# Sums of squares on VectorE alone, and weight pieces split in halves in the first two mixers

## The chip, the core and the metric

The kernel runs on one core of a Trainium2 chip. TensorE does the matrix products (PE in the profile; PEld is its loading of stationary operands), VectorE (DVE), ScalarE (ACT) and GpSimd (POOL) the elementwise work, and SyncE's queue issues the loads. The metric is device microseconds of one execution. The kernel before takes 1027.95 us, the median of 3 runs (1027.83 to 1028.59).

## The reference

Two transformer blocks run one after the other on 256 tokens of width 1024, all in float32. Each has a mixer and a feed-forward part (the second block has two of both), and ahead of each stands an RMS norm:

```
def rmsnorm(x, g):
    return x * lax.rsqrt(jnp.mean(x * x, axis=-1) + EPS) * g

# first block                             # second block
h = h + mixer(rmsnorm(h, g0))             h = h + hgrn2(rmsnorm(h, g0))
u = conv(rmsnorm(h, g1) @ w_up)           h = h + swiglu(rmsnorm(h, g1))
h = h + (silu(gate) * val) @ w_down       h = h + moba(rmsnorm(h, g2))
x = rmsnorm(h, g_final)                   h = h + swiglu(rmsnorm(h, g3))
...
```

The first mixer projects to queries, keys and gates, runs an attention that keeps the 64 best keys of an index score and a latent attention, and merges both through gates. The second is a gated linear recurrence (HGRN2), whose output is normed too; the third is block attention. Widths: the first projection has 3816 columns, the feed-forward inner width is 2816.

## The kernel before

**Tiling.** The residual `h` lies feature-major: 128 partitions by 8 feature blocks by 256 tokens. A product in float32 is made of three products in fp32r: each operand is split into a rounded high part H and the rest L, and H·H, H·L and L·H are summed in PSUM (`mm3`, L511; `proj_w`, L680, does the same with H and L of the tokens side by side, 512 columns). Tokens X, H and L, come from the end of the stage before; weights are split when they have been loaded.

**Weights.** `Weights` (L445) loads a matrix in pieces of up to 1024 elements per partition, 512 KB each. `__getitem__` (L461) splits a whole piece in two instructions: ScalarE copies it to H (`r<-f`, L467), VectorE subtracts H to give L (`r<-f,r`, L468). Pools: 15 raw pieces (`f4`), 23 tiles of H or L (`r4`), so pieces are loaded and split ahead.

**The end of a stage.** `end` (L634) closes each mixer and the first two feed-forward parts. The new values stand in four PSUM banks `accs`, two feature blocks each. Per bank, VectorE adds it to `h` (L650), ScalarE makes X's H (L652) and VectorE X's L (`SCALAR_TENSOR_TENSOR r<-h,vec,r`, or `r<-h,fs,r`, L653). Then `squares` (L571) sums the squares of the eight blocks: ScalarE squares `h` in four tiles of 128x512, and three additions make one tile of them, on GpSimd unless an engine is given. `over_partitions` (L589) folds its two halves (128x256) on the same engine, and eight small TensorE products with `ones` sum over partitions. `mean_rsqrt` (L599) makes 1/rms of it in ten VectorE instructions of 128x2, and `bcast` (L559) spreads it to all partitions: two VectorE instructions `f<-pack,fs`, two TensorE products, a ScalarE copy. The next stage's products use the X that isn't normed yet, and are scaled by 1/rms when they leave PSUM. So TensorE goes on from stage to stage as soon as X is there; the sum and the broadcast stand in its queue among products of the next stage. The end of the convolutional feed-forward part calls `squares` twice (L655, L658): once for the final norm of the first block, and once with its gains, on VectorE, for the first norm of the second block.

**Five such ends** are spoken of below: that of the first mixer (near 195 us), of the first feed-forward part (near 382), of the second mixer (near 529), of the second feed-forward part (near 722) and of the third mixer (near 829). In the second mixer, GpSimd also adds up the squares of the recurrence's output, once for each pair of heads but the first (L1324).

**Order.** The code only records operations (`Trace.add`, L209). `schedule` (L295) then orders them for all engines at once: at each step the engine that is free first takes, of the operations whose inputs are there by a table of prices (`price`, L257), the one recorded first. An operation with `ahead` tiles, such as the split of a weight piece, so fills gaps as long as tiles are free. `nc.floor` (L250) makes every operation recorded while it is set wait for one given operation. Each engine executes its list strictly in order. GpSimd's price is 1000 + 4 ns per element for two inputs, VectorE's 69 + 1.042 (L278 to L288).

Of the kernel before, what the change touches and what calls it, by code (L numbers as in the profile page):

```python
# [9 lines left out]
F32 = mybir.dt.float32  # L10
# [181 lines left out]
class Trace:  # L192
    def __init__(self, nc):
        self.nc, self.ops, self.kinds, self.floor = nc, [], {}, None
        for name in ("tensor", "vector", "scalar", "gpsimd", "sync"):
            setattr(self, name, Engine(self, name))
# [248 lines left out]
class Weights:  # L445
# [15 lines left out]
    def __getitem__(self, k):  # L461
        p = k // self.per
        k0 = p * self.per
        if p not in self.parts:
            nc, raw = self.b.nc, self.fetch(p)
            H, L = (nc.tile("r4", raw.shape, ahead=True) for _ in range(2))
            nc.scalar.activation(H, raw, AF.Copy)  # L467
            nc.vector.tensor_tensor(L, raw, H.bitcast(F32), op=ALU.subtract)  # L468
            self.parts[p] = H, L
        H, L = self.parts[p]  # L470
        return H[:, k - k0, :], L[:, k - k0, :]
# [10 lines left out]
class Builder:  # L482
# [87 lines left out]

    def squares(self, scale=None, eng=None):  # L571

        nc = self.nc
        tot = None
        for i in range(4):
# [7 lines left out]
            if tot is None:  # L583
                tot = sq
            else:
                (eng or nc.gpsimd).tensor_tensor(tot, tot, sq, op=ALU.add)
        return self.over_partitions(tot, eng or nc.gpsimd)

    def over_partitions(self, tot, eng):  # L589

        ss, v = self.ps(2), self.t("f1", SEQ)
        eng.tensor_tensor(v, tot[:, 0], tot[:, 1], op=ALU.add)
        for t in range(2):
# [40 lines left out]
    def end(self, accs, g, scale=None, norm=None):  # L634
# [21 lines left out]
        if norm is not None:  # L656

            ss, v = self.squares(norm, nc.vector), self.t("fs", 2)  # L658
            nc.vector.tensor_tensor(v, r, r, op=ALU.mult)
# [542 lines left out]
    def mixer2(self, X):  # L1202
# [103 lines left out]
        def outs(p, sc, it, og):  # L1306
# [14 lines left out]
            else:  # L1321
                o2 = self.t("f2", 2, SEQ)
                A_.activation(o2, po, AF.Square)
                G.tensor_tensor(sq, sq, o2, op=ALU.add)  # L1324

        for p in range(4):
            sc = scores(p, *front(p))
            outs(p, sc, *sides(p))
        ro = self.bcast(self.mean_rsqrt(self.over_partitions(sq, V)))
        accs = self.new_accs()  # L1330
# [80 lines left out]
def build(tc, a, out, stop=None):  # L1411
    with ExitStack() as ctx:
# [9 lines left out]

        X = b.setup()
        X = b.mixer1(X)
        end = b.nc.last("gpsimd")
        b.late_setup()
# [10 lines left out]
        if stopped("x2"):  # L1437
            return
        X = b.mixer2(X)
        if stopped("h3"):  # L1440
            return
# [33 lines left out]
```

## Time and profile before

The profiled execution took 1028.07 us, its first to last instruction (the span) 1026.3 us.

| | |
|---|---|
| median of 3 runs | 1027.95 us |
| profiled execution | 1028.07 us |
| its span | 1026.3 us |
| TensorE, matrix products busy | 999.1 us, 97% |
| VectorE busy | 774.5 us, 75% |
| ScalarE busy | 577.7 us, 56% |
| GpSimd busy | 42.6 us, 4% |
| granted TensorE clock, mean | 0.999 |

PE's busy time counts products from start to a modelled end, so small gaps are hidden in it; what the table can't tell is when an engine waited and for whom. That is read from the waits and from the order of time in single stretches. Names are the program's, with buffer numbers left out: `ps` is a PSUM bank, `r` a tile of H or L, `f` a float32 tile, `fs` a small one, `h` the residual. All recorded instructions have line 434, so stretches and names tell them apart.

### The profile page before, as it was taken

The numbers are of one execution on the slowest core, as the hardware profiler recorded it, in microseconds if no ns is written. First come the engines' busy times: TensorE is split into PE (matmuls) and PEld (weight loads), VectorE is DVE, ScalarE is ACT, GpSimd is POOL, SyncE is SP. The second block draws the span as 40 slices with busy tenths as digits, with TensorE's granted clock in tenths as the row PEclk, the third lists the DMA queues.
The fourth block names the chain that finished last, engine by engine and source line by source line (L and its number), as shares of the span: only waits on it lengthen the run. The fifth ranks groups of instructions, "written<-read, shape, count | busy, mean of one in ns | idle before, by whom it ended". The sixth has DMA issues, their size and how long they took to land.

```text
span 1026.3 us, 18746 instructions
## 1 busy us (share of the span) xinstructions
PE 999.1 (97%) x7526; PEld 907.1 (88%) x7526; DVE 774.5 (75%) x1434; ACT 577.7 (56%) x960; POOL 42.6 (4%) x41
## 2 busy tenths in 40 slices
PE   7999999999999999999999999999999999999996
PEld 5887899889999998999998999999889988888885
DVE  6998578699888889876878776767846586576774
ACT  7886646556656576444565445455554655545432
POOL 1000000210000002000011000000200020000000
PEclk9999999999999999999999999999999999999999
DMA  9245367377465663644554765657354745556501
GB/s 333 80 145 184 103 190 225 124 242 242 153 207 187 201 199 90 184 146 138 160 178 144 244 192 180 199 171 226 104 161 149 232 148 153 183 176 196 164 1 42
DMA packets 130152, 173.90 MB, mean 169 GB/s; under 512 B 5842, under 2 KB 112730, under 8 KB 129936
## 3 DMA queue, kind: packets, MB, share of 16 engines
q1 hardware_dynamic: 129312, 169.31, 52.5%
q0 software_dynamic: 752, 3.38, 1.0%
q8 instruction: 59, 0.97, 0.4%
q14 instruction: 29, 0.24, 0.1%
HBM read 171.61 MB, written 2.63 MB: 170 GB/s over the span
## 4 chain that ended last, share of the span: by engine, by line
PE 89%; DVE 9%; issue 1%; ACT 1%; DMA 1%; POOL 0%; DVEq 0%; POOLq 0%; ACTq 0%
PE ps L434 89%; DVE r L434 4%; DVE f L434 3%; DVE fs L434 1%; DVE h L434 1%; DMA f<-in_conv_w_dram 1%; ACT f L434 1%; POOL f L434 0%; ACT r L434 0%; DVEq L434 0%; DVE lb L434 0%; POOLq L434 0%; ACTq L434 0%; POOLq L1462 0%
## 5 line engine op out<-in xcount | busy, mean ns | idle before, releaser
L434 PE MATMUL ps<-r,r 128*128 128x256 f32 (+2 forms) x5998 | 926.4, 314 | 8.1 <-DVE r L434 7.5
L434 PEld LDWEIGHTS ps<-r,r 128*128 128x128 f32 x5998 | 834.3, 190 | 81.9 <-DVE r L434 11.1
L434 DVE TENSOR_TENSOR r<-f,r 128x1024 fp32r<-128x1024 f32 (+3 forms) x369 | 414.3, 1150 | 69.6 <-ACT r L434 33.9
L434 ACT ACTIVATE r<-f 128x1024 fp32r<-128x1024 f32 (+3 forms) x373 | 351.1, 980 | 118.9 <-PE ps L434 54.9
L434 ACT ACTIVATE f<-ps 128x256 f32<-128x256 f32 (+5 forms) x226 | 85.5, 424 | 190.5 <-PE ps L434 190.2
L434 DVE TENSOR_TENSOR f<-ps,f 128x256 f32<-128x256 f32 (+1 forms) x178 | 76.0, 460 | 80.5 <-ACT f L434 64.5
L434 DVE TENSOR_TENSOR f<-f,f 128x512 f32<-128x512 f32 (+3 forms) x153 | 100.6, 658 | 12.1 <-ACT f L434 5.5
L434 ACT ACTIVATE f<-f 128x512 f32<-128x512 f32 (+5 forms) x82 | 45.1, 551 | 49.4 <-DVE f L434 48.9
L434 POOL TENSOR_TENSOR f<-f,f 128x512 f32<-128x512 f32 x18 | 26.9, 1494 | 768.5 <-ACT f L434 459.1
L434 DVE SCALAR_TENSOR_TENSOR f<-f,cw,f 128x255 f32<-128x255 f32 (+1 forms) x88 | 38.3, 480 | 10.8 <-ACT f L434 10.7
L434 PE MATMUL ps<-f,f 128*64 128x128 f32 (+4 forms) x320 | 46.3, 330 | 0.1
L434 PEld LDWEIGHTS ps<-f,f 128*64 128x64 f32 (+3 forms) x320 | 35.7, 168 | 6.7 <-issue 2.1
L434 PE MATMUL ps<-pack,f 128*128 128x128 f32 (+2 forms) x165 | 27.5, 293 | 6.5 <-DMA f<-in_conv_w_dram 3.6
L434 ACT ACTIVATE f<-f,fs 128x256 f32<-128x256 f32 (+3 forms) x50 | 24.3, 489 | 16.7 <-DVE fs L434 16.5
L434 ACT ACTIVATE f<-f,vec,cw 128x256 f32<-128x256 f32 x44 | 23.9, 594 | 16.7 <-DVE f L434 16.7
L434 PEld LDWEIGHTS ps<-pack,f 128*128 128x128 f32 (+2 forms) x165 | 20.2, 147 | 11.1 <-DVE f L434 4.8
L434 DVE CUSTOM_DVE_ANT_0 f<-ps,f 128x256 f32<-128x256 f32 (+1 forms) x48 | 17.8, 399 | 14.2 <-PE ps L434 14.1
L434 ACT ACTIVATE f<-ps,fs 128x512 f32<-128x512 f32 (+3 forms) x28 | 15.9, 597 | 19.9 <-PE ps L434 18.8
L434 DVE SCALAR_TENSOR_TENSOR r<-h,vec,r 128x256 fp32r<-128x256 f32 x32 | 23.3, 763 | 2.0 <-ACT r L434 2.0
L434 ACT ACTIVATE r<-h,vec 128x256 fp32r<-128x256 f32 x32 | 14.5, 500 | 15.9 <-DVE h L434 15.9
L434 DVE TENSOR_TENSOR f<-f,fs 128x512 f32<-128x512 f32 (+6 forms) x46 | 16.6, 389 | 7.2 <-PE ps L434 6.7
L434 PEld LDWEIGHTS ps<-f 128*32 128x32 f32 (+2 forms) x880 | 14.0, 114 | 4.3
(85 smaller groups left out, 244.2 us busy)
## 6 DMA issues: line engine op xcount, KB each, us to landing
f<-in_ffn_w_dram SPq DMA_DIRECT2D x132, 512.0 KB, 4.2
f<-in_w_up_dram SPq DMA_DIRECT2D x44, 512.0 KB, 4.7
f<-in_hgrn_w_in_dram SPq DMA_DIRECT2D x32, 512.0 KB, 4.3
f<-in_w_in_dram SPq DMA_DIRECT2D x26, 512.0 KB, 4.9
f<-in_moba_w_in_dram SPq DMA_DIRECT2D x24, 512.0 KB, 4.5
f<-in_w_down_dram SPq DMA_DIRECT2D x22, 512.0 KB, 4.2
f<-in_w_out_dram SPq DMA_DIRECT2D x8, 512.0 KB, 3.9
f<-in_hgrn_w_out_dram SPq DMA_DIRECT2D x8, 512.0 KB, 3.3
```

The costliest lines, as they stand in the source:

```text
L434: getattr(getattr(self.nc, op.eng), op.fn)(*args, **kwargs)
```

## The change

Three things are changed. (1) `squares` and `over_partitions` no longer take an engine: all additions are on VectorE, that of the recurrence's squares too. GpSimd keeps memsets, its DMA issues and one scaling at the very end. (2) In `squares`, the three additions get a floor: they may not come ahead of the last VectorE operation recorded before the call. (3) While `nc.fine` is set, which is in the first and the second mixer, a weight piece is split in two halves on each engine, by rows of the piece where it has more than one, else by columns. The operation that `store_rel` waits for is now the last TensorE operation of the first mixer, not the last GpSimd one.

```diff
     def __getitem__(self, k):
...
             H, L = (nc.tile("r4", raw.shape, ahead=True) for _ in range(2))
-            nc.scalar.activation(H, raw, AF.Copy)
-            nc.vector.tensor_tensor(L, raw, H.bitcast(F32), op=ALU.subtract)
+            if nc.fine:
+                cut = raw.shape[1] > 1
+                n = raw.shape[1] if cut else self.n
+                for c in (slice(0, n // 2), slice(n // 2, n)):
+                    c = (slice(None), c) if cut else (slice(None), slice(None), c)
+                    nc.scalar.activation(H[c], raw[c], AF.Copy)
+                    nc.vector.tensor_tensor(L[c], raw[c], H[c].bitcast(F32), op=ALU.subtract)
+            else:
+                nc.scalar.activation(H, raw, AF.Copy)
+                nc.vector.tensor_tensor(L, raw, H.bitcast(F32), op=ALU.subtract)
...
-    def squares(self, scale=None, eng=None):
+    def squares(self, scale=None):
         nc = self.nc
-        tot = None
+        tot, before = None, nc.last("vector")
...
-                (eng or nc.gpsimd).tensor_tensor(tot, tot, sq, op=ALU.add)
-        return self.over_partitions(tot, eng or nc.gpsimd)
+                nc.floor = before
+                nc.vector.tensor_tensor(tot, tot, sq, op=ALU.add)
+                nc.floor = None
+        return self.over_partitions(tot)
...
-        eng.tensor_tensor(v, tot[:, 0], tot[:, 1], op=ALU.add)
+        self.nc.vector.tensor_tensor(v, tot[:, 0], tot[:, 1], op=ALU.add)
...
-            ss, v = self.squares(norm, nc.vector), self.t("fs", 2)
+            ss, v = self.squares(norm), self.t("fs", 2)
...
-                G.tensor_tensor(sq, sq, o2, op=ALU.add)
+                V.tensor_tensor(sq, sq, o2, op=ALU.add)
...
+        b.nc.fine = True
         X = b.mixer1(X)
-        end = b.nc.last("gpsimd")
+        b.nc.fine = False
+        end = b.nc.last("tensor")
...
+        b.nc.fine = True
         X = b.mixer2(X)
+        b.nc.fine = False
```

In numbers: 23 additions leave GpSimd (18 of 128x512, 5 of 128x256) and come to VectorE; 90 weight pieces are split in 180 instructions on ScalarE and 180 on VectorE (82 of them were 128x1024, 4 128x976, 2 128x768, 2 128x512). TensorE's instructions are the same, in another order.

Since a scheduler sets the order, the diff doesn't show it. Three places do.

First place, VectorE at the end of the first mixer, from the addition of the last bank to `h` (`h_170`); `r_83` there is X's last L, `r<-f,r` are weight pieces, `fs_136<-ps_153` takes the sum of squares. Before:

```order
L434 TENSOR_TENSOR h_170<-ps_154,h_170 128x512
L434 TENSOR_TENSOR r_87<-f_69,r_95 128x1024
L434 SCALAR_TENSOR_TENSOR r_83<-h_170,vec_182,r_83 128x256 x2
L434 TENSOR_TENSOR r_92<-f_65,r_79 128x1024
L434 TENSOR_TENSOR r_81<-f_64,r_80 128x1024
L434 TENSOR_TENSOR f_107<-ps_157,f_116 128x256
L434 TENSOR_TENSOR f_107<-ps_159,f_121 128x256
L434 TENSOR_SCALAR fs_136<-ps_153 128x2
```

Now (`h_170` from `ps_153`, X's last L is `r_81`):

```order
L434 TENSOR_TENSOR h_170<-ps_153,h_170 128x512
L434 TENSOR_TENSOR r_89<-f_64,r_76 128x1024
L434 SCALAR_TENSOR_TENSOR r_81<-h_170,vec_182,r_81 128x256 x2
L434 TENSOR_TENSOR f_109<-f_109,f_103 128x512
L434 TENSOR_TENSOR f_109<-f_109,f_110 128x512
L434 TENSOR_TENSOR r_94<-f_60,r_78 128x1024
L434 TENSOR_TENSOR f_109<-f_109,f_104 128x512
L434 TENSOR_TENSOR f_105<-ps_158,f_123 128x256
L434 TENSOR_TENSOR f_119<-f_109 128x256
L434 TENSOR_TENSOR f_105<-ps_159,f_118 128x256
L434 TENSOR_TENSOR r_87<-f_67,r_90 128x1024
L434 TENSOR_SCALAR fs_136<-ps_160 128x2
```

The three additions and the fold of the halves (`f_119<-f_109`) now stand between X's last L and the sum, with one weight piece among them; GpSimd had them before.

Second place, VectorE at the end of the first feed-forward part, where two sums are made. Before, the second sum's additions (`f_103`) and fold (`f_120`) stood behind X's L, around the first steps of the first 1/rms (`fs_138` to `fs_130`):

```order
L434 TENSOR_TENSOR f_103<-f_103,f_104 128x512
L434 TENSOR_TENSOR r_90<-f_68,r_76 128x1024
L434 TENSOR_TENSOR f_103<-f_103,f_107 128x512
L434 TENSOR_SCALAR fs_138<-ps_159 128x2
L434 TENSOR_TENSOR f_103<-f_103,f_102 128x512
L434 TENSOR_SCALAR fs_148<-fs_138 128x2
L434 TENSOR_TENSOR f_120<-f_103 128x256
L434 TENSOR_TENSOR fs_130<-fs_148 128x2
L434 SCALAR_TENSOR_TENSOR fs_130<-fs_130,fs_138 128x2
L434 SCALAR_TENSOR_TENSOR fs_130<-fs_130 128x2
L434 SCALAR_TENSOR_TENSOR fs_148<-fs_130,fs_148 128x2
L434 TENSOR_TENSOR fs_130<-fs_148 128x2
```

Now the second sum (`f_104`, fold `f_125`) stands behind the end of that 1/rms (`fs_135`), around its broadcast (`f_126`, `f_116` from `pack_174`), and takes `ps_160` after the first products of it:

```order
L434 SCALAR_TENSOR_TENSOR fs_148<-fs_148,fs_138 128x2
L434 SCALAR_TENSOR_TENSOR fs_148<-fs_148 128x2
L434 SCALAR_TENSOR_TENSOR fs_135<-fs_148,fs_135 128x2
L434 TENSOR_TENSOR f_104<-f_104,f_109 128x512
L434 TENSOR_TENSOR fs_130<-fs_135 128x2
L434 TENSOR_SCALAR f_126<-pack_174,fs_135 128x128
L434 TENSOR_TENSOR f_104<-f_104,f_106 128x512
L434 TENSOR_SCALAR f_116<-pack_174,fs_135 128x128
L434 TENSOR_TENSOR f_104<-f_104,f_108 128x512
L434 TENSOR_TENSOR f_125<-f_104 128x256
L434 SCALAR_TENSOR_TENSOR h_170<-h_170,vec_182,f_120 128x256 x2
L434 SCALAR_TENSOR_TENSOR fs_130<-ps_160,fs_130 128x2
```

Third place, VectorE at the start of the first mixer: `r_78` is the L of the first weight piece, `r_77` to `r_81` are X's L, `f_105` and `f_106` the transposed second half of the tokens, `r_84` the second piece. Before:

```order
L434 TENSOR_TENSOR r_78<-f_59,r_76 128x976
L434 TENSOR_TENSOR r_77<-f_103,r_77 128x2x128
L434 TENSOR_TENSOR r_79<-f_103,r_79 128x2x128
L434 TENSOR_TENSOR r_80<-f_104,r_80 128x2x128
L434 TENSOR_TENSOR r_81<-f_104,r_81 128x2x128
L434 TENSOR_TENSOR f_105<-ps_158,vec_182 128x512
L434 TENSOR_TENSOR f_106<-ps_159,vec_182 128x512
L434 TENSOR_TENSOR r_84<-f_61,r_82 128x976
```

Now, from the tokens' second half on (the first half of piece one stands where the whole piece stood, X's four L's of the first half behind it as before):

```order
L434 TENSOR_TENSOR f_105<-ps_158,vec_182 128x512
L434 TENSOR_TENSOR f_106<-ps_159,vec_182 128x512
L434 TENSOR_TENSOR r_78<-f_59,r_76 128x488
L434 TENSOR_TENSOR r_77<-f_105,r_77 128x2x128
L434 TENSOR_TENSOR r_79<-f_105,r_79 128x2x128
L434 TENSOR_TENSOR r_80<-f_106,r_80 128x2x128
L434 TENSOR_TENSOR r_81<-f_106,r_81 128x2x128
L434 TENSOR_TENSOR r_84<-f_61,r_82 128x488 x2
```

The second half of piece one moved behind the transposed second half of the tokens, and piece two behind X's L of it.

## Rows read from the trace of the kernel before

**Rows 1.** The page's first part: busy us of each engine, its share, its instructions.

```profile
PE 999.1 (97%) x7526; PEld 907.1 (88%) x7526; DVE 774.5 (75%) x1434; ACT 577.7 (56%) x960; POOL 42.6 (4%) x41
```

**Rows 2.** Stretches: length, busy of PE, PEld, DVE, ACT, POOL; PEclk, DMA share, GB/s.

```profile
15.50:42.00 26.50, 26.50 (x138) 22.69 (x140) 26.50 (x117) 24.41 (x49) 0.54 (x1) 1.00 0.56 198
42.00:60.50 18.50, 16.23 (x102) 14.02 (x99) 18.36 (x72) 16.90 (x36) 0.00 (x0) 1.00 0.32 94
194.70:210.00 15.30, 13.82 (x95) 11.41 (x93) 14.76 (x27) 8.59 (x16) 6.91 (x6) 1.00 0.28 84
398.00:529.00 131.00, 130.91 (x1799) 124.70 (x1800) 101.85 (x200) 65.25 (x103) 4.50 (x3) 1.00 0.52 161
529.00:542.00 13.00, 11.25 (x66) 9.04 (x66) 12.78 (x18) 8.46 (x15) 5.26 (x4) 1.00 0.25 80
```

**Rows 3.** Waits of PE, then PEld, 190 to 845 us: total, times, longest.

```profile
PE ps L434 <- DVE r L434: 7.0, 7, 1.8
PE ps L434 <- POOL f L434: 0.7, 1, 0.7
PE ps L434 <- DVE f L434: 0.6, 1, 0.6
...
PEld ps L434 <- DVE r L434: 10.2, 10, 2.0
PEld ps L434 <- DVE f L434: 1.6, 4, 0.8
PEld ps L434 <- POOL f L434: 0.9, 1, 0.9
```

**Rows 4.** Timeline at the first mixer's end: start, us, instructions [idle before <-releaser].

```profile
195.31 3.75 DVE L434 SCALAR_TENSOR_TENSOR r<-h,vec,r 128x256 fp32r<-128x256 f32 x4
195.79 2.98 POOL L434 TENSOR_TENSOR f<-f,f 128x512 f32<-128x512 f32 x2 [179.55 <-DVE r L434]
201.24 3.76 PE L434 MATMUL ps<-r,r 128*128 128x512 f32 x19 [1.40 <-DVE r L434]
```

**Rows 5.** Timeline at the second mixer's end, VectorE and GpSimd.

```profile
530.85 0.89 DVE L434 SCALAR_TENSOR_TENSOR r<-h,vec,r 128x256 fp32r<-128x256 f32 x2
533.99 1.91 DVE L434 SCALAR_TENSOR_TENSOR r<-h,vec,r 128x256 fp32r<-128x256 f32 x2
534.09 1.52 POOL L434 TENSOR_TENSOR f<-f,f 128x512 f32<-128x512 f32 x1 [15.55 <-ACT f L434]
```

**Rows 6.** Groups by shape: shapes and count | busy us, mean ns | idle before, releasers.

```profile
L434 DVE TENSOR_TENSOR r<-f,r 128x1024 fp32r<-128x1024 f32 x312 | 380.6, 1238 | 55.5 <-ACT r L434 19.9 <-issue 16.3 <-PE ps L434 16.3
L434 ACT ACTIVATE r<-f 128x1024 fp32r<-128x1024 f32 x312 | 317.9, 1051 | 67.0 <-PE ps L434 54.9 <-issue 11.9
L434 DVE TENSOR_TENSOR f<-f,f 128x512 f32<-128x512 f32 x137 | 95.1, 694 | 12.0 <-ACT f L434 5.5 <-PE ps L434 4.6
L434 POOL TENSOR_TENSOR f<-f,f 128x512 f32<-128x512 f32 x18 | 26.9, 1494 | 768.5 <-ACT f L434 459.1 <-DVE r L434 308.8 <-POOL f L434 0.2
L434 ACT ACTIVATE r<-f 128x512 fp32r<-128x512 f32 x43 | 27.1, 632 | 51.3 <-DVE f L434 51.3
L434 DVE TENSOR_TENSOR f<-f 128x256 f32<-128x256 f32 x6 | 2.5, 422 | 1.2 <-POOL f L434 1.2
```

**Rows 7.** Timeline of VectorE: weight pieces split one behind the other.

```profile
82.01 5.76 DVE L434 TENSOR_TENSOR r<-f,r 128x1024 fp32r<-128x1024 f32 x5
```

**Rows 8.** Timeline, sum of squares to broadcast, after the first mixer.

```profile
206.08 0.14 DVE L434 TENSOR_SCALAR fs<-ps 128x2 f32<-128x2 f32 x1
209.38 0.71 PE L434 MATMUL ps<-f,ones 128*128 128x128 f32 x4
```

**Rows 9.** Timeline of PE, three waits inside the first mixer.

```profile
15.46 11.70 PE L434 MATMUL ps<-r,r 128*128 128x488 f32 x51 [0.52 <-DVE r L434]
50.54 2.82 PE L434 MATMUL ps<-pack,f 128*96 128x128 f32 x24 [1.60 <-DVE f L434]
60.48 0.70 PE L434 MATMUL ps<-pack,f 128*128 128x128 f32 x4 [0.67 <-DVE f L434]
```

More of the change, by code (lines that the diff above doesn't have):

```diff
@@ L193, in __init__ @@
     def __init__(self, nc):
-        self.nc, self.ops, self.kinds, self.floor = nc, [], {}, None
+        self.nc, self.ops, self.kinds, self.floor, self.fine = nc, [], {}, None, False
         for name in ("tensor", "vector", "scalar", "gpsimd", "sync"):
@@ L585, in squares, with over_partitions @@
             else:
-                (eng or nc.gpsimd).tensor_tensor(tot, tot, sq, op=ALU.add)
-        return self.over_partitions(tot, eng or nc.gpsimd)
-    def over_partitions(self, tot, eng):
+                nc.floor = before
+                nc.vector.tensor_tensor(tot, tot, sq, op=ALU.add)
+                nc.floor = None
+        return self.over_partitions(tot)
+    def over_partitions(self, tot):
         ss, v = self.ps(2), self.t("f1", SEQ)
-        eng.tensor_tensor(v, tot[:, 0], tot[:, 1], op=ALU.add)
+        self.nc.vector.tensor_tensor(v, tot[:, 0], tot[:, 1], op=ALU.add)
         for t in range(2):
@@ L1328, in mixer2 @@
             outs(p, sc, *sides(p))
-        ro = self.bcast(self.mean_rsqrt(self.over_partitions(sq, V)))
+        ro = self.bcast(self.mean_rsqrt(self.over_partitions(sq)))
         accs = self.new_accs()
```

## The prediction

> **What bounds the kernel now.** I read the page's first part before anything else. TensorE's products fill 97% of the span and its loads 88%, VectorE 75%, ScalarE 56%, GpSimd 4% [rows 1]: TensorE is the bound, and a change that takes no product away can only win what TensorE waits. So the next view is the table by stretch, to see where those waits are. In the second mixer PE is busy for 130.91 of 131.00 us; at the end of the first mixer it is 13.82 of 15.30, and at the end of the second 11.25 of 13.00, with VectorE busy for 14.76 and 12.78 there [rows 2]. The reader is to see that the gaps sit at the ends of stages, and that VectorE is full at just these places though it is at 75% over all. The third view, who waited for whom, gives them their sum. From 190 us to 845 us, which holds all five ends, the products waited 8.3 us (7.0 for an `r` of VectorE, 0.7 for GpSimd's `f`, 0.6 for VectorE's), and the loads 10.2, 1.6 and 0.9 us for the same three [rows 3]. The load waits are the fuller measure, since a product's end is modelled and covers the start of a gap; of their 1.6 us on VectorE's `f` I count the longest, 0.8, and leave the three short ones, which stand at the broadcasts and stay. So between **8.3 and 11.9 us** of the span are stalls at the five ends.
>
> The last view is the order of time there, to see what makes VectorE late. At the end of the first mixer four `SCALAR_TENSOR_TENSOR r<-h` (X's L) take 3.75 us, and from 0.5 us after their start GpSimd adds for 2.98 us; PE then waits 1.40 us for an `r` [rows 4]. At the end of the second mixer two of them take 0.89 us where GpSimd is idle, and the next two, 3 us later and of the same shape, take 1.91, with an addition of GpSimd (1.52 us) from 0.1 us after their start [rows 5]. So VectorE's instruction is held by about as long as GpSimd's takes: at 0.89 a pair, the four would have taken 1.78, not 3.75. GpSimd's additions are not a help beside VectorE; they stop it while TensorE waits for the next L.
>
> **The change part by part.**
>
> *Additions off GpSimd.* The four L's at the end of the first mixer are done 2.0 us earlier (3.75 less 1.78), which is more than the 1.40 us that PE waited there and about the 1.8 us of the longest load wait. The other ends have the same pattern, and the wait for GpSimd's own `f` (0.7 to 0.9) goes with them. What is late next is TensorE: its products are there. I take the middle of the two measures, **10.1 us won**.
>
> *The same additions on VectorE.* An addition of 128x512 is 0.69 us there against 1.49 on GpSimd, a fold 0.42 [rows 6]: three and one are 2.5 us for a sum, 18 and 5 are 14.6 us in all. The floor puts them behind X's last L, so they can't delay what TensorE waits for first. Queued behind them on VectorE are weight pieces, of which some are ready ahead, and the ten steps of 1/rms. These end in the broadcast, for which PE waits in its order: from the sum to the broadcast's product there were 3.3 us, with one weight piece among them [rows 8]. The new order sets products of the next stage between, enough for a chain of that length by the steps above, but with little to spare. Below nothing I see no reason; above, a whole sum (2.5 us) could come out at each end. I take 0.2 us at each of four ends, which is nearest to their short broadcast waits of before, together 0.8.
>
> *The end with two sums.* There the second sum's additions stood among the first steps of the first 1/rms; now they stand behind its end, so the second broadcast comes later, by up to a sum's 2.5 us. Behind it wait the evictions of the second mixer's first products, not the products themselves, until the broadcast's place in PE's order. Between 0 and 2.5 us; I take 0.4, near the lower end, because one whole projection and most of another stand in PE's order between the two.
>
> *The recurrence's squares.* Three additions of 0.69 us move to VectorE in a stretch where it is busy for 101.85 of 131.00 us and PE waits for nothing [rows 2]. Nothing. If that cover were gone it would be 2.1 us.
>
> *Splitting in halves.* A piece costs VectorE 1.238 us alone, but five in a row take 5.76, so each hides 0.11 behind the one before [rows 6, 7]. Two halves at 0.69 are 1.38 less that overlap, so a split costs 0.03 (1.38 less 0.11 less 1.24) to 0.14 us. On ScalarE it is 2 x 0.632 less 1.051, 0.21, or 0.10 with the same overlap. For 90 pieces this is 3 to 13 us on VectorE and 9 to 19 on ScalarE, beside a TensorE that waits little. It counts only where both engines are full: from 15.5 to 60.5 us VectorE is busy for 44.86 of 45.00 us, and ScalarE for 41.31 [rows 2]. Fourteen pieces are split there in VectorE's order; at 0.06 us each, between the bounds, that is **0.8 us lost**, since PE waits for VectorE at the end of that stretch (1.60 and 0.67 us [rows 9]). Gained at the start: PE's first long run begins after a wait of 0.52 us for the second piece's L [rows 9], and in the new order it has products of both token halves to do before that. I book none of it, because VectorE, not PE, is what is late at 50 us. In the second mixer the halves find no wait to shorten (0.09 us [rows 2]).
>
> The Trainium skill ("Perfetto Trace Analysis", section "Optimizing Scalar/DVE Operations") speaks against the halves: an instruction carries a fixed access cost, about 60 ns on VectorE and 93 on ScalarE in SBUF, and where the engine is saturated larger operations do better. By it fourteen splits would cost 2.1 us if both lay in series, and the sum would end 1.3 us higher.
>
> *The floor of `store_rel`* moves two small loads behind the first broadcast; the one product that needs them stands thirty products further on in PE's order. Nothing, or some tenths.
>
> *Sum.* 10.1 less 0.8 (four broadcasts), 0.4 (two sums) and 0.8 (halves) is 8.1 us. Against the profiled execution's 1028.07 us, 0.12 above the median, that gives **1020.0 us**.
>
> **The rivals.**
>
> *The sum becomes the wait (slower).* Each end's additions, 2.5 us on VectorE, come between X and the broadcast. If PE reaches the broadcast's place sooner than VectorE gets there, it waits by the whole sum at each end, and once more where there are two: six sums, 15 us. Against a gain of 10.1 and with the halves' 0.8 that is 1033.8; at two thirds of it 1028.8. It decides against the change as soon as more than 1.5 us of each sum comes out. For it: GpSimd ran these additions in parallel. Against: VectorE gets back about as much as it is given (2.0 us on four L's alone, against 2.5), and the order was made with VectorE's prices, which are near its durations.
>
> *The halves take it back.* The first mixer is bound by VectorE to 60 us, and a new order there may cost what it likes: at the upper bounds fourteen splits are 2.0 us on VectorE and 2.9 on ScalarE, 4.9 in series, 4.1 more than booked: **1024.1 us**. For it: 44.86 of 45.00. Against: PE has other products to fill with in the new order.
>
> *The halves gain too.* If the earlier first half moves the whole chain, the waits of 0.52, 1.60 and 0.67 us [rows 9] go, 2.8 us: **1017.2 us**. Against: VectorE has more to do there, not less.
>
> *The change doesn't do what it says.* If X's L's are slow for another reason, say because ScalarE's H comes late, taking GpSimd away frees only the 0.7 to 0.9 us that PE waited for GpSimd itself, and the time stays at **1027**. Against: rows 5, the same instruction at both speeds a few us apart.
>
> **How the numbers follow.** Chances: forecast 0.62, halves take it back 0.15, halves gain 0.10, the sum becomes the wait 0.07, no effect 0.06. The range reaches down to all load waits won with some of the start's 0.52 (1028.07 less 11.9 less 0.5, 1015.7), and up to the smaller measure with the two-sum end at its bound and half of the halves' 4.9 (8.3 less 0.8, 2.5 and 2.5 is 2.5: 1025.5): 1015.5 to 1025.5. It holds the forecast's case, the second and most of the third. A measurement of this kernel can tell about 0.2%, 2 us, from no change, so below 1025.9 counts as faster: 0.85 (forecast, most of the second case, the third); within 2 us of before 0.09; slower 0.06.
>
> **What would show it.** In the trace of the changed kernel, the four L's at the first mixer's end should take some 1.7 us, not 3.75, the waits of PE for `r` at the five ends should be near nothing (below 2 us together, from 8.3), and GpSimd should have no additions. New waits would stand at the broadcasts (`f<-pack,fs` as releaser) if the sum is late. From 10 us to 95 us the trace should be at most 1 us longer. Wrong is the prediction if the L's are as slow as before, if the broadcasts wait over 1 us each, or if the first mixer's end moves by more than 2 us either way.

## The result and the profile after

The changed kernel takes **1019.08 us** (median of 4 runs, 1018.50 to 1019.43) where the kernel before takes 1028.15 beside it: a ratio of 0.991, 95% interval 0.9896 to 0.9923. It is 9.1 us faster; 1020.0 was predicted, with a range of 1015.5 to 1025.5. The total came out as forecast, but two terms of the sum were mis-sized in opposite directions, and the experiments below are mostly about these.

The first part of the page of the changed kernel (busy us, share, instructions), and its chain by engine:

```profile
PE 1000.9 (98%) x7526; PEld 909.1 (89%) x7526; DVE 775.2 (76%) x1547; ACT 584.2 (57%) x1050; POOL 9.4 (1%) x18
...
PE 97%; DVE 1%; DMA 1%; ACT 0%; issue 0%; POOLq 0%
```

Against [rows 1], VectorE is busy for 0.7 us more although it does 113 instructions more, GpSimd for 33 us less. The same stretches as [rows 2], in the changed kernel (length, then busy time and count of PE, PEld, DVE, ACT, POOL, then clock, DMA share, GB/s):

```profile
15.50:42.00 26.50, 26.50 (x127) 22.13 (x125) 26.02 (x127) 24.82 (x62) 1.06 (x2) 1.00 0.55 188
42.00:60.50 18.50, 18.46 (x107) 15.58 (x107) 18.50 (x65) 17.36 (x36) 0.00 (x0) 1.00 0.35 114
194.70:210.00 15.30, 15.30 (x113) 13.81 (x112) 14.49 (x27) 9.01 (x17) 0.68 (x2) 1.00 0.40 126
398.00:529.00 131.00, 130.79 (x1809) 124.15 (x1808) 104.56 (x233) 66.26 (x130) 0.00 (x0) 1.00 0.50 161
529.00:542.00 13.00, 13.00 (x94) 11.36 (x93) 12.72 (x23) 8.90 (x17) 0.00 (x0) 1.00 0.22 66
```

At the two stage ends PE is now busy for the whole stretch (15.30 of 15.30, 13.00 of 13.00), and does 113 and 94 products there, before 95 and 66. Note the second row: PE is "busy" for 18.46 us instead of 16.23, with only five products more. Each product counts from its start to its modelled end, so a slow row can look full: 32 products of 64x256 take 5.93 us there, one every 0.185, without an idle time between them, where before 16 took 2.00, one every 0.125. This row says nothing of progress; the times at which things happen, further down, do.

The waits from 190 to 845 us [rows 3]: for the products there is no row left at all. For the loads (total, times, longest) there are these two:

```profile
PEld ps L434 <- issue: 1.4, 4, 0.6
PEld ps L434 <- DVE f L434: 0.6, 2, 0.4
```

The waits for VectorE's `r` and for GpSimd's `f` are gone, and all but 0.6 us of those for VectorE's `f`: 8.3 us by the products, 12.1 by the loads (10.2, 1.6 and 0.9, less the 0.6 left). The time line at the first mixer's end, VectorE's four L's (answering [rows 4]) and PE up to the broadcast (answering [rows 8]):

```profile
198.02 1.71 DVE L434 SCALAR_TENSOR_TENSOR r<-h,vec,r 128x256 fp32r<-128x256 f32 x4
...
207.38 0.16 DVE L434 TENSOR_SCALAR fs<-ps 128x2 f32<-128x2 f32 x1
...
206.41 0.31 PE L434 MATMUL ps<-ones,f 128*32 128x1 f32 x16
206.64 7.27 PE L434 MATMUL ps<-r,r 128*128 128x256 f32 x41
213.75 0.61 PE L434 MATMUL ps<-f,ones 128*128 128x128 f32 x4
```

Four L's take 1.71 us, before 3.75. From the sum to the broadcast's product there are now 6.4 us (207.38 to 213.75), before 3.3, yet nothing waits: 41 products stand between, and none of these rows has an idle time in brackets. At the second mixer's end [rows 5] both pairs now take the same:

```profile
529.32 0.88 DVE L434 SCALAR_TENSOR_TENSOR r<-h,vec,r 128x256 fp32r<-128x256 f32 x2
...
532.46 0.88 DVE L434 SCALAR_TENSOR_TENSOR r<-h,vec,r 128x256 fp32r<-128x256 f32 x2
```

Over the whole run, all 32 L's of this form lie between 476 and 488 ns; before, between 472 and 1604. The groups by shape that answer [rows 6] (count | busy us, mean ns | idle before):

```profile
L434 DVE TENSOR_TENSOR r<-f,r 128x1024 fp32r<-128x1024 f32 x230 | 276.1, 1220 | 59.2 <-PE ps L434 22.6 <-ACT r L434 20.7 <-issue 14.4
L434 ACT ACTIVATE r<-f 128x1024 fp32r<-128x1024 f32 x230 | 233.7, 1051 | 59.7 <-PE ps L434 53.6 <-issue 6.1
L434 DVE TENSOR_TENSOR r<-f,r 128x512 fp32r<-128x512 f32 x201 | 132.6, 687 | 15.4 <-ACT r L434 15.1
L434 DVE TENSOR_TENSOR f<-f,f 128x512 f32<-128x512 f32 x155 | 106.7, 689 | 10.5 <-ACT f L434 6.7 <-PE ps L434 1.4
```

82 whole pieces are gone and 162 halves of 512 have come (other halves are smaller), at the price that [rows 6] gave for a half, and the 18 additions that VectorE took over cost 0.69 us each, as booked.

**What went the other way** is the first mixer. Its landmarks in the changed kernel (PE's first group with conv_w's transposes; VectorE's MAX8, which carry the choice of keys, with shortest, median and longest ns and first and last start; a wait of PE behind them; the first addition to h at the end):

```profile
8.01 2.44 PE L434 MATMUL ps<-pack,f 44*128 44x44 f32 x11 [4.57 <-DMA f<-in_conv_w_dram]
...
L434 DVE MAX8 fs<-f x16: 404/419/425, 53.7 to 80.5; 128x8 f32<-128x256 f32 x16
...
98.28 0.70 PE L434 MATMUL ps<-pack,f 128*128 128x128 f32 x4 [0.81 <-DVE f L434]
...
194.53 0.69 DVE L434 TENSOR_TENSOR h<-ps,h 128x512 f32<-128x512 f32 x1 [1.00 <-PE ps L434]
```

The same four in the kernel before:

```profile
7.00 2.44 PE L434 MATMUL ps<-pack,f 44*128 44x44 f32 x11 [3.59 <-DMA f<-in_conv_w_dram]
...
L434 DVE MAX8 fs<-f x16: 406/420/433, 47.4 to 78.1; 128x8 f32<-128x256 f32 x16
...
95.43 0.70 PE L434 MATMUL ps<-pack,f 128*128 128x128 f32 x4 [0.61 <-DVE f L434]
...
191.82 0.69 DVE L434 TENSOR_TENSOR h<-ps,h 128x512 f32<-128x512 f32 x1 [1.00 <-PE ps L434]
```

The first mixer's end comes 2.7 us later. Of this 1.0 us is there from the start: PE waits for the transfer of conv_w and goes on at 7.00 us in one execution and at 8.01 in the other, and both kernels wait for it alike. Counted from there, the first mixer takes 184.82 us before and 186.52 after: **1.7 us lost**. The first MAX8 comes 5.3 us later by the same count, the last 1.4.

### The profile page after: what moved, and what is told of

Its sections match the earlier page's. It is cut to its first block, busy times and chain, and to the rows that moved or that the text cites. A ratio compares the mean times of both kernels' runs of the same rounds, so it can differ in the third digit from the quotient of the medians.

```text
span 1017.7 us, 18892 instructions
## 1 busy us (share of the span) xinstructions
PE 1000.9 (98%) x7526; PEld 909.1 (89%) x7526; DVE 775.2 (76%) x1547; ACT 584.2 (57%) x1050; POOL 9.4 (1%) x18
## 4 chain that ended last, share of the span: by engine, by line
PE 97%; DVE 1%; DMA 1%; ACT 0%; issue 0%; POOLq 0%
PE ps L434 97%; DMA f<-in_conv_w_dram 1%; DVE f L434 0%; DVE fs L434 0%; ACT f L434 0%; ACT r L434 0%; DVE r L434 0%; POOLq L1477 0%
## 5 line engine op out<-in xcount | busy, mean ns | idle before, releaser
L434 ACT ACTIVATE r<-f 128x1024 fp32r<-128x1024 f32 (+3 forms) x463 | 359.0, 827 | 114.5 <-DVE f L434 54.5
L434 DVE TENSOR_TENSOR f<-f,f 128x512 f32<-128x512 f32 (+4 forms) x171 | 112.3, 658 | 10.6 <-ACT f L434 6.7
L434 PE MATMUL ps<-f,f 128*64 128x128 f32 (+4 forms) x320 | 49.3, 332 | 0.2
L434 ACT ACTIVATE f<-f,fs 128x256 f32<-128x256 f32 (+3 forms) x50 | 24.3, 488 | 16.9 <-DVE fs L434 16.8
L434 PE MATMUL ps<-f 128*32 128x16 f32 (+3 forms) x880 | 17.7, 191 | 0.0
L434 DVE SCALAR_TENSOR_TENSOR r<-h,vec,r 128x256 fp32r<-128x256 f32 x32 | 14.3, 482 | 2.1 <-ACT r L434 2.1
```

Source lines behind the costliest of these rows:

```text
L434: getattr(getattr(self.nc, op.eng), op.fn)(*args, **kwargs)
```

## The experiments

The theory was the prediction's: GpSimd's additions hold VectorE's instructions that read two operands from SBUF, and at the stage ends TensorE waits for these; the halves cost a little where VectorE is full. The rivals were that GpSimd was only a slow link in the chain, and that the halves gain, or take much back.

**The additions alone.** The halves are left out.

```diff
-        b.nc.fine = True
         X = b.mixer1(X)
-        b.nc.fine = False
...
-        b.nc.fine = True
         X = b.mixer2(X)
-        b.nc.fine = False
```

> The changed kernel without the halves: all additions of squares on VectorE, every weight piece split by one instruction per engine. The theory of the prediction (the additions earn the time at the stage ends, the halves cost some 0.8 us): 1018.3 us, ratio to before 0.990. Rival, the halves take much back (up to 1.6 us of the first mixer's loss between 98 and 112 us, and as much in the second): 1015.5 to 1017.5. Rival, the halves gain too: 1021 to 1023.

1017.15 us (1017.09 to 1017.34), before 1028.84, ratio 0.9886 (0.9872 to 0.9899). The additions earn 11.7 us, and the halves take 1.9 of them back (1019.08 less 1017.15). The intervals allow some 1.5 us either way, but the traces say the same: counted from conv_w's transposes to the last instruction, the kernel before takes 1019.3 us, this one 1007.6 and the changed one 1009.6, so 11.7 are earned and 2.1 taken back.

They are also earned where they were looked for. From the first addition to h at one end to that at the next, the trace here is 2.0, 2.6, 2.7 and 1.8 us shorter, and 2.1 behind the fifth end; the load waits at these ends were 2.0, 2.8, 3.3, 1.7 and 2.0 us.

The first mixer, from conv_w's transposes to the first addition to h, takes 184.83 us here, as before the change:

```profile
7.54 2.45 PE L434 MATMUL ps<-pack,f 44*128 44x44 f32 x11 [4.07 <-DMA f<-in_conv_w_dram]
...
192.37 0.69 DVE L434 TENSOR_TENSOR h<-ps,h 128x512 f32<-128x512 f32 x1 [1.00 <-PE ps L434]
```

So the loss in the first mixer belongs to the halves.

**The halves alone**, in the kernel before:

```diff
+        b.nc.fine = True
         X = b.mixer1(X)
+        b.nc.fine = False
```

and the same around the second mixer, with the changed way to split a piece; GpSimd keeps its additions.

> The kernel before with the halves in the first two mixers, the additions left on GpSimd. The theory of the prediction: 1028.9 us (0.8 more than before), ratio 1.000 to 1.002, and VectorE's four L's at the first mixer's end still take 3.7 us or so. Rival, the halves take much back: 1030 to 1032. Rival, the halves gain: 1024 to 1027.

1034.09 us (1033.82 to 1035.46), ratio 1.0053 (1.0041 to 1.0066): 5.3 us slower than before, more than any theory had. The first mixer gives 1.3 of it (186.15 us by the count above). The rest is at the end of the first feed-forward part (the first ffn's end below), whose own pieces are whole, but where VectorE splits the second mixer's ahead; and it shows the other side of the contention. VectorE (part of its row), GpSimd and PE there:

```profile
392.15 0.68 DVE L434 TENSOR_TENSOR f<-f,f 128x512 f32<-128x512 f32 x1
392.75 0.87 DVE L434 SCALAR_TENSOR_TENSOR r<-h,fs,r 128x256 fp32r<-128x256 f32 x2
393.55 0.68 DVE L434 TENSOR_TENSOR r<-f,r 128x512 fp32r<-128x512 f32 x1
...
396.89 0.68 DVE L434 TENSOR_TENSOR r<-f,r 128x512 fp32r<-128x512 f32 x1
...
393.23 5.47 POOL L434 TENSOR_TENSOR f<-f,f 128x512 f32<-128x512 f32 x1 [2.88 <-issue]
398.78 0.72 POOL L434 TENSOR_TENSOR f<-f 128x256 f32<-128x256 f32 x1
...
399.56 0.39 PE L434 MATMUL ps<-ones,f 128*32 128x1 f32 x16 [3.03 <-POOL f L434]
...
406.90 0.61 PE L434 MATMUL ps<-f,ones 128*128 128x128 f32 x4
```

From 391.6 to 397.6 us VectorE runs one instruction with two SBUF operands behind the other, the new halves among them, each at its own price (0.68 us). GpSimd's addition, 1.5 us long in the mean [rows 6], begins at 393.23 and ends 5.47 us later, 1.1 us after VectorE's row has stopped. So the hold goes both ways: a GpSimd addition can hold VectorE, and a row of VectorE can keep GpSimd out. What decides is not shown: at 387.22 us of the same trace an addition began inside such a row, took 1.43 us, and the half beside it 1.79. PE waits 3.03 us for the sum, and the first broadcast's product stands at 406.90, in the kernel before at 400.70: 6.2 us later, of which 0.9 were there when this end began (383.25 against 382.31).

Behind that wait the granted clock drops. The windows (columns as above, the clock is the third number from the end):

```profile
398.00:402.00 4.00, 2.44 (x39) 2.20 (x40) 1.81 (x9) 0.86 (x2) 1.42 (x2) 0.70 0.14 50
402.00:406.00 4.00, 4.00 (x21) 4.00 (x20) 2.87 (x15) 0.00 (x0) 0.00 (x0) 0.50 0.43 131
```

0.50 is 1.2 GHz, the lower of the two levels: 21 products in 4 us, where the same stretch at 1.00 holds 36 (below). It is a small part of the 5.3 us: the profiled execution has a mean clock of 0.994 and is 0.7 us above the median. Three others have 0.997, which the clock's fall in the last 5 us of the kernel explains by itself, and they take 1033.8 to 1034.1. The fifth has 0.996 and is 1.4 us above the median.

**GpSimd additions that nobody waits for**, put back beside VectorE's at the stage ends:

```diff
+                nc.floor = nc.last("scalar")
+                if scale is None:
+                    self.extra(ks)
                 nc.floor = before
                 nc.vector.tensor_tensor(tot, tot, sq, op=ALU.add)
...
+    def extra(self, ks):
+        nc, d = self.nc, self.t("dm", 2, SEQ)
+        nc.gpsimd.tensor_tensor(d, self.h[:, ks, :], self.h[:, ks, :], op=ALU.add)
```

> The changed kernel plus 15 additions on GpSimd that nobody waits for: three at each of the five stage ends that had them, each reads h twice (128x512) and writes a scratch tile that is not read, and starts when the square of its part is done. The order of instructions on the other four engines is that of the changed kernel. If GpSimd's reads of SBUF hold VectorE's two-input instructions (the theory), the L's at the ends go from 0.48 us to 0.8 us or more each in the mean and 4 to 8 us of the gain are lost: 1023 to 1027 us. If GpSimd was only a slow link of the chain (rival), nothing waits for these and the time stays at 1018.5 to 1020.

1026.38 us (1025.76 to 1027.60), ratio 0.9975 (0.9966 to 0.9984): 7.3 us of the gain are lost again. The instructions of the other four engines stand in the order of the changed kernel, and nothing depends on these additions, so the rival falls as the whole account: GpSimd needs to be late for nobody to cost the time. The rows show how: the L's (shortest, median and longest ns, first and last start), the first end, and the products' wait there:

```profile
L434 DVE SCALAR_TENSOR_TENSOR r<-h,vec,r x32: 470/476/1262, 195.4 to 833.7; 128x256 fp32r<-128x256 f32 x32
...
197.54 2.48 DVE L434 SCALAR_TENSOR_TENSOR r<-h,vec,r 128x256 fp32r<-128x256 f32 x4
...
196.62 2.32 POOL L434 TENSOR_TENSOR dm<-h 128x512 f32<-128x512 f32 x2 [178.45 <-DVE h L434]
...
202.98 1.19 PE L434 MATMUL ps<-r,r 128*128 128x512 f32 x4 [0.93 <-DVE r L434]
```

My number for the mean of an L (0.8 us or more) was too high for all of them: the median stays at 0.476, and only the L's that meet an addition are held, by up to 0.8 us. How the other 4.4 of the additions' 11.7 us divide, the run doesn't say: its additions start at other times, and TensorE waited 0.7 to 0.9 us for GpSimd itself [rows 3].

**GpSimd writes instead of reads.** Each of these additions becomes three memsets of the scratch tile.

```diff
-        nc.gpsimd.tensor_tensor(d, self.h[:, ks, :], self.h[:, ks, :], op=ALU.add)
+        for _ in range(3):
+            nc.gpsimd.memset(d, 0.0)
```

> The same with three GpSimd memsets of the scratch tile (128x512, some 0.5 us each, no reads) in place of each of the 15 additions. If it is the reads of SBUF that hold VectorE: no loss, 1018.5 to 1020 us, L's at 0.48 us. If any GpSimd work that touches SBUF holds VectorE: a loss like that with the reads, 1023 to 1027.

1018.99 us (1018.49 to 1019.47), but this run tells nothing: the floor orders instructions within the program, and nothing on the chip held the memsets back. They ran at 17.8 us (nine) and at 232.9 us (36), far from any L. So the same with a tie to h, a GpSimd addition of two columns ahead of each three memsets:

```diff
+        a = self.h[:, ks.start, :2]
+        nc.gpsimd.tensor_tensor(d[:, 0, :2], a, a, op=ALU.add)
         for _ in range(3):
             nc.gpsimd.memset(d, 0.0)
```

> In the run with the memsets the trace shows them at 17.8 and 232.9 us, far from the stage ends: nothing that the chip waits for held them. Here each group of three memsets of the scratch tile (128x512, no reads) comes behind a GpSimd addition of two columns of h, which does wait for its part of h, so that the writes stand beside the L's. If it is the reads of SBUF that hold VectorE: 1018.5 to 1020.5 us, the L's that lie beside memsets at 0.48 us. If any GpSimd work on SBUF holds VectorE: 1023 to 1027.

1018.32 us (1017.75 to 1018.72), ratio 0.9896 (0.9881 to 0.9911). The rows at the first end, and all L's:

```profile
197.26 1.71 DVE L434 SCALAR_TENSOR_TENSOR r<-h,vec,r 128x256 fp32r<-128x256 f32 x4
...
196.69 1.69 POOL L434 MEMSET dm<- 128x512 f32 x3
198.47 0.20 POOL L434 TENSOR_TENSOR dm<-h 128x2 f32<-128x2 f32 x1
198.72 1.70 POOL L434 MEMSET dm<- 128x512 f32 x3
...
L434 DVE SCALAR_TENSOR_TENSOR r<-h,vec,r x32: 473/477/485, 195.1 to 826.0; 128x256 fp32r<-128x256 f32 x32
```

With memsets running beside it, the row of four L's takes 1.71 us, as in the changed kernel, and the memsets 0.57 each. It is GpSimd's reading that holds VectorE, not its work as such. The Trainium skill ("SBUF — State Buffer", section "Who interferes with whom") states just this: a VectorE instruction with two SBUF inputs contends with a GpSimd instruction that reads SBUF, not with one that only writes it, and the order of issue decides who blocks. The runs agree with the first, 1026.38 against 1018.32 us. For the second they show both outcomes, VectorE held in one run and GpSimd in another, but not what decides.

**The halves in one mixer.** With all additions on VectorE, the flag is left on around the first mixer alone, then around the second alone.

> All additions on VectorE, the halves in the first mixer alone. By the traces the 1.9 us that the halves cost beside VectorE's additions are lost in the first mixer (between 98 and 112 us): 1019.0 us. Rival, a cost per instruction in both mixers: 1018.1.

> All additions on VectorE, the halves in the second mixer alone. If the first mixer pays: 1017.2 us, like the run without halves. Rival, a cost per instruction in both mixers: 1018.1. Rival, the halves gain there: under 1016.5.

1018.34 us (ratio 0.9897, 0.9881 to 0.9914) and 1017.33 (0.9887, 0.9872 to 0.9902): 1.2 and 0.2 us more than without halves. The first is nearer to the rival's 1018.1 than to my 1019.0, but the second isn't: most of what the halves cost is in the first mixer (186.36 us by the count above; 184.81 with halves in the second mixer alone). It is not lost between 98 and 112 us, as I had it: in the changed kernel 1.4 us have come by the last MAX8, at 80.5. The intervals allow some 1.5 us either way, so I rely on that count, which lies between 184.80 and 184.83 in the five kernels whose first mixer has no halves and the same start, and between 186.13 and 186.87 in the eight that have them.

**Price or order?** Each piece is split by two halves that stand one behind the other in the place of the whole one, so that no engine's order changes:

```diff
-                args = [real(v) for v in op.args]
-                ...
+                for c in op.half or (None,):
+                    args = [real(v[c] if c and isinstance(v, View) else v) for v in op.args]
+                    ...
```

> All additions on VectorE; in the first two mixers each weight piece is split by two half-size instructions that stand one right behind the other in the place of the whole one, so the order of all engines is that of e1_adds. If what the halves cost (1.9 us) is the price of the instructions in the full stretch: the first mixer's end 1.3 to 1.6 us later than in e1_adds, counted from the conv_w transposes, and 1018.5 to 1019.2 us. If it is the new order that the halves bring: 1017.2 us or less.

1017.83 us (1017.52 to 1018.08), ratio 0.9894 (0.9879 to 0.9909): 0.7 us above the kernel without halves, 1.25 below the changed one. Neither theory's number. The first mixer takes 186.55 us, as long as in the halves' own order, but for another reason (the first line is from the kernel without halves):

```profile
51.07 2.82 PE L434 MATMUL ps<-pack,f 128*96 128x128 f32 x24 [1.55 <-DVE f L434]
...
51.36 4.49 PE L435 MATMUL ps<-pack,f 128*96 128x128 f32 x24 [2.27 <-DVE f L435]
...
53.00:54.00 1.00, 1.00 (x7) 0.95 (x6) 1.00 (x6) 0.74 (x2) 0.00 (x0) 0.50 0.05 16
```

The wait that was 1.55 us without halves is 2.27, the 0.7 us that I had booked as the halves' price. Behind it the clock falls to 0.50 for 3.4 us, and the 24 transposes take 4.49 us instead of 2.82. Two of the four executions have a mean clock of 0.996 and two of 0.999, and the latter take 1017.5 and 1017.6, some 0.4 us more than without halves.

The first MAX8, ahead of the fall, comes 0.97 us later than without halves by the same count, 0.07 for each of fourteen pieces. So the price of the instructions is 0.4 to 1.0 us, by the measure. The rest of the 1.9 goes with the new order; that is what is left over, not a run of its own.

In the changed kernel VectorE, from conv_w's transposes to the last MAX8, is busy for 68.41 us (68.04 without halves) of 72.49 (71.06): of 1.4 us more, 0.4 is work and 1.1 is VectorE idle. Most of that idle time is in three rows, which the trace without halves doesn't have:

```profile
13.55 0.69 DVE L434 TENSOR_TENSOR f<-ps,vec 128x512 f32<-128x512 f32 x1 [0.38 <-PE ps L434]
14.41 0.69 DVE L434 TENSOR_TENSOR f<-ps,vec 128x512 f32<-128x512 f32 x1 [0.16 <-PE ps L434]
...
37.90 0.56 DVE L434 TENSOR_TENSOR f<-f,fs 128x128 f32<-128x128 f32 x3 [0.43 <-ACT f L434]
```

The first two are the third place of the change: VectorE waits for the transposes of the tokens' second half, with the second half of piece one set behind them.

A rival inside this one is untested. TensorE starts slowly: in the changed kernel its products of 128x488 follow one another every 0.41 us up to 16.7 us and every 0.22 us from 17 us on, in the kernel without halves every 0.22 us from 13.4 us on, but for its waits. This change of pace, from the lower level of the clock to the upper, stands in every trace's record of the granted clock. It comes 7.0 to 9.6 us after conv_w's transposes in the seven kernels with the halves' own order, and 4.0 to 6.0 us after them in the five without halves there and in this run. Of the seven, the three with 7.0 to 7.5 us take 186.13 to 186.18 us for the first mixer, the four with 8.6 to 9.6 take 186.36 to 186.87. So some tenths of the loss go with a later clock; which is the cause of which is not shown.

**The halves alone, with one sum moved.** The kernel with halves and GpSimd's additions, but the first sum at the first ffn's end on VectorE:

```diff
-        r = self.mean_rsqrt(self.squares())
+        r = self.mean_rsqrt(self.squares(eng=None if norm is None else nc.vector))
```

> The halves beside GpSimd's additions (e2_halves), with the additions of the sum at the first ffn's end alone moved to VectorE. In e2_halves TensorE waits 3.0 us for GpSimd there and the granted clock falls to 0.50 from 399.6 to 406.4 us. If that wait, and the clock behind it, are most of the 5.3 us lost: 1027 to 1029 us, no wait for GpSimd at that end, clock 1.00 there. Rival, the halves cost it elsewhere: 1031 to 1034.

1027.47 us (1026.64 to 1028.04), ratio 0.9987 (0.9979 to 0.9996): this one sum is worth 6.6 us beside the halves. PE has no wait left between 380 and 470 us; there the kernel before waits 2.4 us, so some 4.2 of the 6.6 are the halves' loss at this end, which is about what the first mixer had left over of the 5.3. The window that held 21 products above is now

```profile
402.00:406.00 4.00, 4.00 (x36) 4.00 (x35) 3.67 (x15) 3.07 (x7) 0.00 (x0) 1.00 0.56 182
```

So the rest of the loss was at that end, by the sum that GpSimd couldn't finish, and, as the executions at 0.997 say, by the late chain far more than by the clock.

**The recurrence's three additions back on GpSimd**, and **no floor under VectorE's additions**, each from the kernel without halves:

```diff
-                V.tensor_tensor(sq, sq, o2, op=ALU.add)
+                G.tensor_tensor(sq, sq, o2, op=ALU.add)
```

> The run without halves (e1_adds), with the recurrence's three additions of squares (second mixer, at some 453, 487 and 517 us) back on GpSimd. The prediction booked nothing for these three: 1017.2 us, within 0.5 of e1_adds. Rival, they too hold VectorE where TensorE waits: 1018 to 1020. Rival, they lie better on GpSimd: under 1016.5.

```diff
-                nc.floor = before
                 nc.vector.tensor_tensor(tot, tot, sq, op=ALU.add)
-                nc.floor = None
```

> The run without halves (e1_adds), without the rule that an addition may stand no earlier than behind the last VectorE instruction written before the sums; the additions then stand earlier among the L's at the first and third ends. If the place of the additions on VectorE matters, TensorE waits for r again at the ends and the time is 1018 to 1021 us. Rival, VectorE has room enough: 1017.2.

1016.61 us (1015.95 to 1017.27) and 1016.97 (1016.45 to 1017.41), against 1017.15: neither can be told from it. The three additions in mid-recurrence cost nothing on either engine, since TensorE waits for nothing there, and VectorE has room for the sums at the places that both runs tried (without the floor, one addition stands ahead of the last L's at the first end).

**conv_w's transposes out of the way**, from the kernel without halves. They are put behind the hundredth instruction of TensorE:

```diff
+        nc.floor = [op.i for op in nc.ops if op.eng == "tensor"][100]
         for j in range(3):
             nc.tensor.transpose(ps[:, j * 44:(j + 1) * 44], rows[:, j, :], self.ident[:44, :44])
+        nc.floor = None
```

> All additions on VectorE, no halves, and the three transposes of conv_w put behind the hundredth instruction of TensorE, out of the way of x's transposes. In the trace TensorE waits for the DMA of conv_w until 8.0 us, with x's transposes behind it. If x is there by then: 1 to 3 us won, 1014 to 1016 us. Rival, x's own transfer or the first piece of W is as late: 1017 us.

**1016.09 us** (1016.07 to 1016.31), ratio 0.9875 (0.9860 to 0.9890), the fastest of all by the median: 3.0 us less than the changed kernel. PE's start:

```profile
5.23 1.97 PE L434 MATMUL ps<-pack,f 128*128 128x128 f32 x8 [1.79 <-DMA f<-in_x_dram]
8.27 0.78 PE L434 MATMUL ps<-r,r 128*128 128x488 f32 x1 [1.08 <-ACT r L434]
```

x's transposes now start at 5.23 us, not behind conv_w's transfer at 7 to 8, and the first mixer's end comes 1.5 us earlier than in the kernel without halves (190.83 against 192.37). 1.1 us of that is left in the total; it also takes the chance out of the start, which moved by up to 1.3 us with the landing of conv_w from one profile to another.

## Why the prediction was right, and where it wasn't

**What bounds the kernel** was read rightly: what TensorE waited at the five ends was to be had, and nearly all of it went.

**The mechanism** stands, with more behind it than rows 4 and 5 gave. The same instruction at two speeds with GpSimd beside it was a coincidence in time, until additions on GpSimd that nobody waits for brought 7.3 us of the loss back and its writes alone didn't. The rival that X's L's were late for another reason is out.

**The term "10.1 us won"** was too small. The step that failed is "I take the middle of the two measures". The load waits, 11.9 us, were the right one: the additions alone earn 11.7, with every cost that they brought to VectorE already in it, and end by end the trace agrees to 0.6 us. (`store_rel`'s new floor, booked at nothing, is in this number and wasn't tried by itself.)

**The two costs beside it**, 0.8 at four broadcasts and 0.4 at the end with two sums, don't show. At the first mixer the time from the sum to the broadcast doubled, from 3.3 us to 6.4, just as the prediction feared, and 41 products covered it. At the end with two sums the second broadcast came at 409.51 us, before at 404.98, with 64 products unbroken ahead of it. The order held more cover than I counted. With these, ends and sums came to 11.7 where 8.9 was booked.

**The recurrence's squares** at nothing: right, by the run that puts them back.

**The halves** at 0.8 us were booked too small: 1.9. The price per instruction was about right (0.4 to 1.0 us where only the price changes, and 0.7 on the wait where it shows), and so was the place, the first mixer, with little in the second (0.2 by the medians, 0.35 by the traces). Two of its readings were slightly off: of the fourteen pieces two are split before 15.5 us, and the 1.238 us of a whole piece hold some that GpSimd had stretched (1.220 in the changed kernel). The step that failed is that the price was taken as the whole cost, though the pieces also change places: the rival "the halves take it back" named that ("a new order there may cost what it likes") but priced it by the upper bounds of the instructions. The Trainium skill's fixed costs ("Perfetto Trace Analysis", "Optimizing Scalar/DVE Operations") gave 2.1 us for fourteen splits in series, close to the 1.9, but the runs don't bear out the reason: the same splits in place cost 0.4 to 1.0 us, which is VectorE's part (0.07 for each by the first MAX8) and not both engines' one behind the other.

**The signs to look for.** The L's at 1.7 us (1.71), the waits for `r` near nothing (none), no additions on GpSimd and no waits at the broadcasts: all as told. Two were not: between 10 and 95 us the trace should have been at most 1 us longer, and it is 2.9 (95.43 to 98.28), 1.0 of it from the start; and I had called the prediction wrong if the first mixer's end moved by more than 2 us. It moved by 2.7, of which 1.7 are the halves'. By that sign the halves' step is wrong, and so it is.

That the forecast lies 0.9 us from the time is luck in part: 2.8 us too little were booked as won at the ends and 1.1 too little as lost by the halves, and the two errors work against each other.

## What to carry to other kernels

Work that is moved to an idle engine is not free if both engines read two operands from the same memory at the same time: look for one instruction shape that runs at two speeds, and for what runs beside the slow ones. A helper that only writes can stay. Where two measures of the same wait differ, ask which of them covers the start of the gap; here the loads' did. And when a change splits instructions under a scheduler, price the new order as a risk of its own, since the added price of the instructions was only a part of what they cost.

## What the runs showed of the hardware that was not expected

The hold between VectorE and GpSimd goes both ways, and it can last for a row: behind seven VectorE instructions with two SBUF operands and no gap, a GpSimd addition of 1.5 us took 5.47. It need not, as the addition at 387.22 us of the same trace shows, which held VectorE from inside such a row. A 128x2 GpSimd addition, 0.20 us at its shortest, took 0.60 and 0.75 beside two-operand instructions of VectorE at the first ffn's end (with the memsets, 386.36 and 388.80 us).

An instruction of VectorE that reads one operand from SBUF and the other from PSUM isn't held: the additions to h (`h<-ps,h`) that ran beside GpSimd's additions, at 386.36 us in the kernel before and at 196.93 us in the run with the reads, took 0.68 and 0.69 us, as everywhere.

TensorE's clock fell from its upper to its lower level in the midst of the kernel in two of the profiles, both times behind a wait: 0.50 from 399.6 to 406.4 us behind a wait of 3.03 us, and from 52.0 to 55.4 us behind one of 2.27. After the waits of 1.4 to 1.8 us in the kernel before it stayed at 1.00. So a longer wait can cost more than itself; between executions of one kernel with a lower and a higher mean clock the difference was 0.5 us in one case and 0.7 to 1.4 in the other. At the start the profile prints 1.00 too, but the record of the clock begins only at 16.8 us in the changed kernel, and up to there the products ran at the pace of the lower level (0.41 us from one 128x488 to the next, then 0.22).
